# A seven-product block multiply on TensorE: two of the seven products in two matmuls per row block instead of three, and the sums of weights earlier

## Chip, cores, metric

The kernel runs on one core of a Trainium2 chip. The metric is the device time of one launch in microseconds, the median of several runs.

## What is computed

One decoder block in float32: a pre-norm, an input projection, latent attention and a gated spatial unit side by side, their gated sum, an output projection, and a SwiGLU feed-forward layer. Cut to the parts that the change touches, the products with the input projection's `u` and gate columns and with the two feed-forward weights:

```python
a = rms_norm(h, norm_mix_g[l])
z = a @ w_in[l]                 # 512 x 2048 times 2048 x 7232
...
f = rms_norm(h, norm_ffn_g[l])
h = h + (jax.nn.silu(f @ w_gate_ffn[l]) * (f @ w_up_ffn[l])) @ w_down_ffn[l]   # width 5632
```

## The kernel before

**Precision.** A float32 operand is split into a high part (rounded to the type `fp32r`, which TensorE multiplies in one pass) and a low part (the remainder). A product is then three matmuls: low weights by high data, high by high, high by low, summed in one PSUM bank.

**Units.** For `u`, the two gates, and the feed-forward gate and up weights, the work is cut into units of 256 output features by 512 tokens over 2048 inputs. A unit halves all three dimensions and does seven products of quarter size instead of eight (Strassen's scheme in Winograd's form). `Unit` (from line 400) holds a unit's weights `a11, a12, a21, a22`. For product `i`, `weights(i)` makes the sum or difference of quarters that it needs (`plus` and `minus`, lines 392 and 395, VectorE, 128x1024) and `form_w` splits it: ScalarE writes the high part (line 372), VectorE the low part (line 373). `multiply(i)` runs the product: `product` (lines 378 to 386) goes over 8 blocks of 128 rows, three matmuls of 256 columns each, 24 in a product. The data `x` of a block lies as 512 columns, high part first, low part behind it.

**Banks.** A unit has three PSUM banks of 512 columns, of which 256 are used. Products 0 to 6 add into banks 0, 1, 2, 1, 0, 1, 2. Between products, `read(i)` takes the sums so far:

- read 0: ScalarE copies bank 0 into `u` (line 398). Read 1: VectorE adds bank 1 and `u` into `u2` (line 392), before product 3 adds to bank 1 again.
- read 3: two VectorE adds, of bank 1 and of bank 2, into `c22`. Read 4: a ScalarE copy of bank 0. Read 5: an add of bank 1. Read 6: an add of bank 2, and then the unit is finished: SiLU for a gate unit of the feed-forward part (a multiply of two tiles on VectorE at line 908, the activation on ScalarE at line 909), a multiply with the gate for an up unit (line 916), an activation on ScalarE alone in the first run.

**Order.** `run` (from line 465) writes the order out by hand, and `pin` keeps it on each engine. Step `g` of the loop stands for product `g`: first `read` of product `g - 4`, then `weights` of product `g`, then `multiply` of product `g - 3`. So the weights are three products ahead of TensorE, and the reads one behind. Steps run on over the units: the reads of products 3 to 6 of a unit fall beside the weights of products 0 to 3 of the next. There are 20 units in the first run (4 of `u`, 8 pairs of the two gates) and 44 in the second (22 pairs of feed-forward gate and up).

**Buffers.** `Arena` (from line 46) hands out pieces of two large tiles, `af` (float32) and `ar` (the split parts), by rules of least recent use. The sum `s1` of a unit is a piece of `af` from product 1 to product 3.

Of the kernel before, what the change touches and what calls it, by code (L numbers as in the profile page):

```python
# [88 lines left out]
def tile_block(ctx: ExitStack, tc, a):  # L89
    nc = tc.nc  # L90
# [8 lines left out]
    def T():  # L99
        return af.get(2)  # L100

    def drop(*ts):

        for t in ts:
            if isinstance(t, (tuple, list)):
                drop(*t)
            elif id(t) in af.held:
                af.put(t)
            else:
                ar.put(t)  # L110

    def PS():
        return psp.tile([P, 512], F32, tag="b", name="b")
# [183 lines left out]
    kps = PS()  # L297
    for half in range(2):
# [5 lines left out]
        for k in range(8):  # L304
            w = wk[:, k].rearrange("p o m -> p (o m)")
# [61 lines left out]
    pin = tc.keep_in_program_order  # L367

    def form_w(src):
        hi, lo = ar.get(4), ar.get(4)  # L370
        hv, lv = (t.rearrange("p (k m) -> p k m", m=P) for t in (hi, lo))
        pin(nc.scalar.copy(hv, src))  # L372
        pin(nc.vector.tensor_tensor(out=lv, in0=src, in1=hv.bitcast(F32), op=ALU.subtract))  # L373
        return hi, lo

    FORM = (0, 5, 6, 4, 1, 2, 3)

    def product(ps, w, xs, kps, first):
        hi, lo = w
        for kp in kps:  # L380
            x = xs[kp]
            ks = slice(kp * P, (kp + 1) * P)
            xh, xl = x[:, :256], x[:, 256:]
            pin(nc.tensor.matmul(ps, lo[:, ks], xh, start=first and kp == 0, stop=False, skip_group_check=True))  # L384
            pin(nc.tensor.matmul(ps, hi[:, ks], xh, start=False, stop=False, skip_group_check=True))  # L385
            pin(nc.tensor.matmul(ps, hi[:, ks], xl, start=False, stop=kp == 7, skip_group_check=True))  # L386

    def bank():
        return PS()[:, :256]

    def plus(out, in0, in1):
        pin(nc.vector.tensor_tensor(out=out, in0=in0, in1=in1, op=ALU.add))  # L392

    def minus(out, in0, in1):
        pin(nc.vector.tensor_tensor(out=out, in0=in0, in1=in1, op=ALU.subtract))  # L395

    def copy(out, t):
        pin(nc.scalar.copy(out, t))  # L398

    class Unit:  # L400
# [8 lines left out]
            self.finish = finish  # L409

        def weights(self, i):
            if i == 0:
                return form_w(self.a11)
            if i == 1:
                self.st = af.get(4)
                self.s1 = self.st.rearrange("p (k m) -> p k m", m=P)
                plus(self.s1, self.a21, self.a22)
                minus(self.a21, self.a11, self.a21)
                minus(self.a11, self.s1, self.a11)
                return form_w(self.a11)  # L420
            if i == 2:
                return form_w(self.a21)
            if i == 3:
                w = form_w(self.s1)
                drop(self.st)
                return w
            if i == 4:
                return form_w(self.a12)
            if i == 5:
                minus(self.a12, self.a12, self.a11)  # L430
                return form_w(self.a12)
            w = form_w(self.a22)
            drop(self.raw)
            return w

        def multiply(self, i, w, fx, kps):
            if i == 0 and 0 in kps:
                self.banks = [bank() for _ in range(3)]
            n = FORM[i]
            xs = [f[n] if isinstance(f, list) else f[:, n * 512:(n + 1) * 512] for f in fx]  # L440
            product(self.banks[(0, 1, 2, 1, 0, 1, 2)[i]], w, xs, kps, i < 3)

        def read(self, i):
            ba, bb, bd = self.banks
            if i == 0:
                self.out = T(), T()
                self.u = T(), T()
                copy(self.u[0][:, :256], ba)
            u, u2 = self.u[0][:, :256], self.u[1][:, :256]
            (c11, c12), (c21, c22) = ((t[:, :256], t[:, 256:]) for t in self.out)  # L450
            if i == 1:
                plus(u2, bb, u)
            elif i == 3:
                plus(c22, bb, u)
                plus(c22, bd, c22)
            elif i == 4:
                copy(c11, ba)
            elif i == 5:
                plus(c12, bb, u)
            elif i == 6:  # L460
                plus(c21, bd, u2)
                drop(self.u)
                self.finish(self.out)

    def run(jobs, fx, rest, ends, lead=3):


        af.keep, af.pack = 32, True
        jobs = list(jobs)
        last = 7 * len(jobs) - 7  # L470
        units, ready = {}, {}

        def unit(n):
            if n < len(jobs):
                units[n] = Unit(*jobs[n])

        unit(0)
        for g in range(last + 7 + lead + 1):
            g1, g2 = g - lead, g - lead - 1
            if g2 >= 0:  # L480
                units[g2 // 7].read(g2 % 7)
            if g < last + 7:
                ready[g] = units[g // 7].weights(g % 7)
                if g % 7 == 6:
                    unit(g // 7 + 2)
            if g == lead - 1:
                rest = rest()
                next(rest)
                early = len(fx)
                for i in range(lead):  # L490
                    units[0].multiply(i, ready[i], fx, range(early))
                for _ in rest:
                    pass
                unit(1)
            if 0 <= g1 < last + 7:
                if g1 == last:
                    fx[:] = [ar.cut(f, 2) for f in fx]
                units[g1 // 7].multiply(g1 % 7, ready[g1], fx, range(early if g1 < lead else 0, len(fx)))
                drop(ready.pop(g1))
                if g1 >= last:  # L500
                    drop([f[FORM[g1 - last]] for f in fx])
                    if g1 - last in ends:
                        ends[g1 - last]()
        af.keep, af.pack, ar.keep = 0, False, 0
# [28 lines left out]
    def x_rest():  # L533
# [5 lines left out]

    latT, zs = [], []  # L540
    run(x_jobs(), fx, x_rest, {0: lambda: zs.append(lat_in(0)), 2: lambda: zs.append(lat_in(1)),
                               4: lambda: latT.append(latents(0, zs[0])), 5: lambda: latT.append(latents(1, zs[1]))})
    qnT, kvT = latT
# [119 lines left out]
    def k_proj(pr):  # L663
        ch = [chunk(a["w_ukv"][pr, c]) for c in range(2)]
        ks = []
        for m in range(2):
            ps = PS()
            for k in range(4):
                hi, lo = ch[k // 2]
                o = (k % 2) * 512 + m * P  # L670
                mm3(ps, hi[:, o:o + P], lo[:, o:o + P], *kvT[k], k == 0, k == 3)
            ks.append(split(ps))
        return ks, ch
# [63 lines left out]
    def values(e, pts, vs):  # L737
        ps = PS()
        for j, (ph, pl, q0) in enumerate(pts):
            vh, vl = vs[j // 2]  # L740
            o = (j % 2) * 256 + e * P
            mm3(ps[:, q0:], vh[:, o:o + P], vl[:, o:o + P], ph, pl, j == 0, j == NB - 1)
        return ps
# [15 lines left out]
    ks, ch = k_proj(0)  # L759
    vs = v_proj(ch)  # L760
    for pr in range(NP):
        prob, ptiles = scores(qs, qp, ks)
        if pr + 1 < NP:
            qs, qp = q_proj(pr + 1)
            ks, ch = k_proj(pr + 1)
# [12 lines left out]
        for e in range(2):  # L778
            ps = values(e, pts[e][1], vs)
            t = T()  # L780
# [60 lines left out]
    for c in range(4):  # L841
# [30 lines left out]
        if c == 0:  # L872
# [3 lines left out]
            for tb in range(NB):  # L876
                t = T()
# [56 lines left out]
    def split_hidden():  # L934
        hid[:4] = [move(t) for t in hid[:4]]

    run(ffn_jobs(), ff, f_rest, {1: lambda: hid.extend(hidden_in(0, 4)), 4: split_hidden,
                                 5: lambda: hid.extend(hidden(4, 4))})

# [32 lines left out]
    for c in range(4):  # L972
        t = T()
# [3 lines left out]
    for tb in range(NB):  # L977
        ts = slice(tb * P, (tb + 1) * P)
        for c in range(4):
            ps = PS()  # L980
            for k in range(4):
                xh, xl = hid[k]
# [6 lines left out]
        for c in range(4):  # L989
            t = h[tb][c]  # L990
# [87 lines left out]
```

## Time and profile before

| | |
|---|---|
| median of three runs | 2737.75 us (2736.56 to 2738.42) |
| the profiled execution | 2731.94 us |
| its span, first to last instruction | 2729.9 us |
| TensorE matmul busy | 2679.5 us, 98% of the span, 17320 matmuls |
| VectorE busy | 1731.3 us, 63% |
| ScalarE busy | 1093.6 us, 40% |
| mean granted TensorE clock | 0.993 |
| matmuls of lines 384, 385, 386 | 3584 each, mean 284 ns |
| other matmuls of the same kind, lines 169 to 171 | 2016 each, mean 379 to 380 ns |

The profile's times come from one profiled execution, so a sum made from them is set against 2731.94 us and then carried to the median. Busy time of an engine counts overlapping instructions once. A matmul's own duration holds its way through the array, and the next one starts before it ends: what a matmul costs in a stream is read from one start to the next. In a list of instructions the bracket at the end of a row is idle time of the engine just before it, and what ended it.

### The profile page before, as it was taken

To read this page: it belongs to the slowest core of one execution; us is meant where nothing else is said; L and a number is where in the kernel's file an instruction comes from. 1 tells how busy PE (TensorE), PEld (TensorE's weight loads), DVE (VectorE), ACT (ScalarE), POOL (GpSimd) and SP (SyncE) were. 2 spreads that over 40 slices of the span, in tenths; PEclk is the share of its full clock that TensorE was granted. 3 is DMA by queue.
4 is the path that set the end of the run, shared out by engine and by line. 5 is a ranking of instruction groups with operands and counts; after the bars stand their busy time and mean duration, and the time that the engine had idled before them with its cause. 6 is when DMAs were issued, how large, how long until landed. Compare 5 with 4: busy or idle time off the path is not lost.

```text
span 2729.9 us, 41675 instructions
## 1 busy us (share of the span) xinstructions
PE 2679.5 (98%) x17320; PEld 2458.8 (90%) x17320; DVE 1731.3 (63%) x2200; ACT 1093.6 (40%) x1534; POOL 201.4 (7%) x377
## 2 busy tenths in 40 slices
PE   8999999999899999999999999999999999999998
PEld 6879999998789878888799999999999998888887
DVE  5647777787677433333687887887888875344434
ACT  6334444457456422233544443444444343222212
POOL 1000000011101220001000000000000020000000
PEclk9999999999999999999999999999999999999999
DMA  7433343343423754334233232332322356334321
GB/s 300 150 125 114 119 146 125 130 144 129 139 86 124 250 188 147 120 112 139 101 123 118 110 131 109 131 111 107 140 109 109 132 170 224 123 123 132 112 89 62
DMA packets 104540, 365.22 MB, mean 134 GB/s; under 512 B 14304, under 2 KB 14304, under 8 KB 104352
## 3 DMA queue, kind: packets, MB, share of 16 engines
q1 hardware_dynamic: 72720, 260.60, 27.2%
q0 software_dynamic: 30192, 99.38, 10.6%
q8 instruction: 135, 2.21, 0.3%
q10 hardware_dynamic: 1440, 2.60, 0.3%
q14 instruction: 53, 0.43, 0.1%
HBM read 317.17 MB, written 45.35 MB: 133 GB/s over the span
## 4 chain that ended last, share of the span: by engine, by line
PE 82%; issue 9%; DMA 4%; DVE 3%; ACT 1%; POOL 1%; SPq 0%; POOLq 0%; ACTq 0%; DVEq 0%
PE b L384 15%; PE b L386 15%; PE b L385 15%; PE b L169 12%; PE b L171 12%; PE b L170 12%; DMA af<-in_xT 1%; DVE ar L373 1%; DMA af<-in_w_uq 1%; ACT ar L372 1%; DVE af L395 0%; PE b L732 0%; DVE af L392 0%; DMA sgd<-af 0%; DMA af<-in_w_lat 0%
## 5 line engine op out<-in xcount | busy, mean ns | idle before, releaser
L384 PE MATMUL b<-ar 128*128 128x256 f32 x3584 | 1017.6, 284 | 6.6 <-ACT ar L333 3.4
L386 PE MATMUL b<-ar 128*128 128x256 f32 x3584 | 1017.2, 284 | 5.4 <-DVE ar L119 5.4
L385 PE MATMUL b<-ar 128*128 128x256 f32 x3584 | 1016.5, 284 | 0.0
L169 PE MATMUL b<-ar 128*128 128x512 f32 (+1 forms) x2016 | 766.3, 380 | 25.3 <-ACT ar L154 11.6
L171 PE MATMUL b<-ar 128*128 128x512 f32 (+1 forms) x2016 | 763.8, 379 | 0.3 <-DVE ar L155 0.3
L170 PE MATMUL b<-ar 128*128 128x512 f32 (+1 forms) x2016 | 764.0, 379 | 0.0
L373 DVE TENSOR_TENSOR ar<-af,ar 128x1024 fp32r<-128x1024 f32 x448 | 543.2, 1223 | 267.9 <-ACT ar L372 266.9
L384 PEld LDWEIGHTS b<-ar 128*128 128x128 f32 x3584 | 690.5, 193 | 7.9 <-DVE af L392 4.0
L386 PEld LDWEIGHTS b<-ar 128*128 128x128 f32 x3584 | 690.5, 193 | 6.3 <-DVE ar L119 6.3
L385 PEld LDWEIGHTS b<-ar 128*128 128x128 f32 x3584 | 690.7, 193 | 0.1
L372 ACT CAST ar<-af 128x1024 fp32r<-128x1024 f32 x448 | 458.5, 1047 | 479.8 <-DVE af L395 367.9
L155 DVE TENSOR_TENSOR ar<-af,ar 128x1024 fp32r<-128x1024 f32 (+1 forms) x224 | 268.2, 1204 | 423.5 <-ACT ar L154 347.4
L169 PEld LDWEIGHTS b<-ar 128*128 128x128 f32 x2016 | 380.5, 189 | 97.6 <-ACT ar L154 11.9
L171 PEld LDWEIGHTS b<-ar 128*128 128x128 f32 x2016 | 380.2, 189 | 71.5 <-DVE ar L155 1.5
L170 PEld LDWEIGHTS b<-ar 128*128 128x128 f32 x2016 | 380.6, 189 | 69.6
L154 ACT CAST ar<-af 128x1024 fp32r<-128x1024 f32 (+1 forms) x224 | 230.0, 1036 | 503.0 <-PE b L170 241.6
L395 DVE TENSOR_TENSOR af<-af 128x1024 f32<-128x1024 f32 x192 | 234.6, 1222 | 4.3
L392 DVE TENSOR_TENSOR af<-b,af 128x256 f32<-128x256 f32 x320 | 134.3, 420 | 14.3 <-PE b L386 12.1
L137 ACT CAST ar<-af 128x512 fp32r<-128x512 f32 x100 | 59.6, 620 | 180.1 <-PE b L170 43.7
L398 ACT COPY af<-b 128x256 f32<-128x256 f32 x128 | 47.4, 370 | 178.8 <-PE b L386 132.5
L138 DVE TENSOR_TENSOR ar<-af,ar 128x512 fp32r<-128x512 f32 x100 | 67.2, 687 | 71.5 <-ACT ar L137 67.7
L942 DVE SCALAR_TENSOR_TENSOR af<-b,rest,af 128x512 f32<-128x512 f32 x96 | 71.3, 748 | 44.5 <-PE b L171 44.5
(223 smaller groups left out, 1193.5 us busy)
## 6 DMA issues: line engine op xcount, KB each, us to landing
af<-in_w_gate SPq DMA_DIRECT2D x88, 512.0 KB, 4.9
af<-in_w_up SPq DMA_DIRECT2D x88, 512.0 KB, 5.3
af<-in_w_down SPq DMA_DIRECT2D x88, 512.0 KB, 3.5
af<-in_w_g SPq DMA_DIRECT2D x64, 512.0 KB, 5.4
af<-in_w_oattn SPq DMA_DIRECT2D x32, 512.0 KB, 4.2
af<-in_w_out SPq DMA_DIRECT2D x32, 512.0 KB, 3.5
hidd<-af POOLq DMA_DIRECT2D x44, 256.0 KB, 2.6
af<-hidd POOLq DMA_DIRECT2D x44, 256.0 KB, 3.6
```

What stands on the lines that cost most here:

```text
L154: nc.scalar.copy(hi[:, :n], raw[:, :n])
L155: nc.vector.tensor_tensor(out=lo[:, :n], in0=raw[:, :n], in1=hi[:, :n].bitcast(F32), op=ALU.subtract)
L169: nc.tensor.matmul(ps, sl, mh, start=first, stop=False)
L170: nc.tensor.matmul(ps, sh, mh, start=False, stop=False)
L171: nc.tensor.matmul(ps, sh, ml, start=False, stop=last)
L372: pin(nc.scalar.copy(hv, src))
L373: pin(nc.vector.tensor_tensor(out=lv, in0=src, in1=hv.bitcast(F32), op=ALU.subtract))
L384: pin(nc.tensor.matmul(ps, lo[:, ks], xh, start=first and kp == 0, stop=False, skip_group_check=True))
L385: pin(nc.tensor.matmul(ps, hi[:, ks], xh, start=False, stop=False, skip_group_check=True))
L386: pin(nc.tensor.matmul(ps, hi[:, ks], xl, start=False, stop=kp == 7, skip_group_check=True))
L392: pin(nc.vector.tensor_tensor(out=out, in0=in0, in1=in1, op=ALU.add))
L395: pin(nc.vector.tensor_tensor(out=out, in0=in0, in1=in1, op=ALU.subtract))
```

## The change

For bank 2 (products 2 and 6) `product` takes the high weights once for both parts of the data, in one matmul of 512 columns, and then the low weights for the high part, 256 columns: two matmuls for a row block in place of three. The bank then holds two halves that have to be added, which `add`, new, does with one more VectorE add in read 3 and one in read 6. `u` and `u2` become the halves of one tile `us`. In `weights`, the three sums for products 1 to 3 are made in the step of product 0, and the difference for product 5 in the step of product 4, behind that step's split.

```diff
+    WIDE = (False, False, True)
+
+    def product(b, ps, w, xs, kps, first):
...
+            start, stop = first and kp == 0, kp == 7
+            if WIDE[b]:
+                pin(nc.tensor.matmul(ps, hi[:, ks], x, start=start, stop=False, skip_group_check=True))
+                pin(nc.tensor.matmul(ps[:, :256], lo[:, ks], xh, start=False, stop=stop, skip_group_check=True))
+            else:
+                ps = ps[:, :256]
...
         def weights(self, i):
...
             if i == 0:
-                return form_w(self.a11)
-            if i == 1:
+                w = form_w(self.a11)
                 self.st = af.get(4)
                 self.s1 = self.st.rearrange("p (k m) -> p k m", m=P)
                 plus(self.s1, self.a21, self.a22)
                 minus(self.a21, self.a11, self.a21)
                 minus(self.a11, self.s1, self.a11)
...
+            w = form_w((None, self.a11, self.a21, self.s1, self.a12, self.a12, self.a22)[i])
             if i == 3:
-                w = form_w(self.s1)
                 drop(self.st)
...
-            if i == 5:
+            elif i == 4:
                 minus(self.a12, self.a12, self.a11)
-                return form_w(self.a12)
...
+        def add(self, out, b, t=None):
+
+            ps = self.banks[b]
+            if t is not None:
+                plus(out, ps[:, :256], t)
+            if t is None and not WIDE[b]:
+                copy(out, ps[:, :256])
+            elif t is None:
+                copy(out, ps[:, 256:])
+                plus(out, ps[:, :256], out)
+            elif WIDE[b]:
+                plus(out, ps[:, 256:], out)
...
             if i == 0:
-                self.out = T(), T()
-                self.u = T(), T()
-                copy(self.u[0][:, :256], ba)
+                self.out, self.us = (T(), T()), T()
...
             elif i == 3:
-                plus(c22, bb, u)
-                plus(c22, bd, c22)
+                self.add(c22, 1, u)
+                self.add(c22, 2, c22)
...
             elif i == 6:
-                plus(c21, bd, u2)
-                drop(self.u)
+                self.add(c21, 2, u2)
+                drop(self.us)
```

In the changed file the wide matmul is line 389 and its narrow partner line 390, the other three are lines 393 to 395, `plus` is line 398, `minus` 401, `copy` 404.

TensorE, in a unit of the first run, from the end of product 1 to the start of product 2. `b_` with a number is a PSUM bank, `ar` holds the split parts. Before:

```order
L384 MATMUL b_2083<-ar_66 128x256
L385 MATMUL b_2083<-ar_66 128x256
L386 MATMUL b_2083<-ar_66 128x256
L384 MATMUL b_2084<-ar_66 128x256
L385 MATMUL b_2084<-ar_66 128x256
L386 MATMUL b_2084<-ar_66 128x256
```

and with the change:

```order
L393 MATMUL b_2027<-ar_66 128x256
L394 MATMUL b_2027<-ar_66 128x256
L395 MATMUL b_2027<-ar_66 128x256
L389 MATMUL b_2028<-ar_66 128x512
L390 MATMUL b_2028<-ar_66 128x256
```

Product 1 is as it was; a row block of product 2 is one matmul of 512 columns and one of 256.

VectorE, one turn of the loop in the first run, from the low forms of products 3 and 4 of a unit (`ar<-af,ar`) to read 6 of the same unit. Rows `af<-b,af` are adds out of PSUM, rows `af<-af` sums of weights. Before:

```order
L373 TENSOR_TENSOR ar<-af,ar 128x1024 x2
L392 TENSOR_TENSOR af<-b,af 128x256
L395 TENSOR_TENSOR af<-af 128x8x128
L373 TENSOR_TENSOR ar<-af,ar 128x1024 x2
L392 TENSOR_TENSOR af<-b,af 128x256 x2
L373 TENSOR_TENSOR ar<-af,ar 128x1024
L392 TENSOR_TENSOR af<-af 128x1024
L395 TENSOR_TENSOR af<-af 128x8x128 x2
L373 TENSOR_TENSOR ar<-af,ar 128x1024
L392 TENSOR_TENSOR af<-b,af 128x256
L373 TENSOR_TENSOR ar<-af,ar 128x1024
L392 TENSOR_TENSOR af<-b,af 128x256
```

and with the change:

```order
L373 TENSOR_TENSOR ar<-af,ar 128x1024 x2
L401 TENSOR_TENSOR af<-af 128x8x128
L398 TENSOR_TENSOR af<-b,af 128x256
L373 TENSOR_TENSOR ar<-af,ar 128x1024 x2
L398 TENSOR_TENSOR af<-b,af 128x256 x3
L373 TENSOR_TENSOR ar<-af,ar 128x1024
L398 TENSOR_TENSOR af<-af 128x1024
L401 TENSOR_TENSOR af<-af 128x8x128 x2
L373 TENSOR_TENSOR ar<-af,ar 128x1024
L398 TENSOR_TENSOR af<-b,af 128x256
L373 TENSOR_TENSOR ar<-af,ar 128x1024
L398 TENSOR_TENSOR af<-b,af 128x256 x2
```

The subtraction for product 5 and the add of read 1 have changed places; read 3 is three adds instead of two, read 6 two instead of one. The three sums of weights stand where they stood.

## Rows read from the trace of the kernel before

**Rows 1.** Busy time in 1400 to 2250 us: length, PE, PEld, DVE, ACT, POOL, clock, DMA.

```profile
1400.00:2250.00 850.00, 850.00 (x7053) 848.58 (x7053) 676.38 (x762) 354.57 (x431) 34.08 (x64) 1.00 0.34 123
```

**Rows 2.** Waits of the whole run: us in total, times, longest.

```profile
PE b L384 <- DVE af L392: 3.2, 3, 2.0
...
PE b L169 <- DVE nm L712: 9.5, 2, 7.7
...
ACT af L398 <- DVE ar L373: 43.3, 19, 3.6
```

**Rows 3.** TensorE in order of time, first run: start, duration; 49 matmuls left out.

```profile
599.78 0.28 PE L384 MATMUL b<-ar 128*128 128x256 f32 x1
...
605.78 0.28 PE L386 MATMUL b<-ar 128*128 128x256 f32 x1
```

**Rows 4.** The same in a stretch of 512 columns; 17 matmuls left out.

```profile
1099.74 0.39 PE L170 MATMUL b<-ar 128*128 128x512 f32 x1
...
1103.82 0.39 PE L170 MATMUL b<-ar 128*128 128x512 f32 x1
```

**Rows 5.** The same in attention, where the sizes change.

```profile
664.24 0.40 PE L169 MATMUL b<-ar 128*128 128x512 f32 x1
664.47 0.40 PE L170 MATMUL b<-ar 128*128 128x512 f32 x1
...
665.46 0.28 PE L169 MATMUL b<-ar 128*128 128x256 f32 x1
665.57 0.28 PE L170 MATMUL b<-ar 128*128 128x256 f32 x1
```

**Rows 6.** TensorE at an up unit: last matmul of one product 3, first of the next.

```profile
1970.89 0.28 PE L386 MATMUL b<-ar 128*128 128x256 f32 x1
...
1988.30 0.28 PE L384 MATMUL b<-ar 128*128 128x256 f32 x1
```

**Rows 7.** VectorE in the same stretch.

```profile
1971.21 0.88 DVE L392 TENSOR_TENSOR af<-b,af 128x256 f32<-128x256 f32 x2
1972.29 1.23 DVE L373 TENSOR_TENSOR ar<-af,ar 128x1024 fp32r<-128x1024 f32 x1 [0.20 <-ACT ar L372]
...
1980.95 0.41 DVE L392 TENSOR_TENSOR af<-b,af 128x256 f32<-128x256 f32 x1
...
1984.20 2.44 DVE L373 TENSOR_TENSOR ar<-af,ar 128x1024 fp32r<-128x1024 f32 x2 [1.64 <-ACT ar L372]
1986.56 0.42 DVE L392 TENSOR_TENSOR af<-b,af 128x256 f32<-128x256 f32 x1
1986.89 1.22 DVE L395 TENSOR_TENSOR af<-af 128x1024 f32<-128x1024 f32 x1
```

**Rows 8.** VectorE and TensorE in the first up unit, where product 3 waited.

```profile
1382.93 0.42 DVE L392 TENSOR_TENSOR af<-b,af 128x256 f32<-128x256 f32 x1
...
1382.43 0.28 PE L386 MATMUL b<-ar 128*128 128x256 f32 x1
1383.40 0.38 PE L384 MATMUL b<-ar 128*128 128x256 f32 x1 [0.69 <-DVE af L392]
1383.62 0.28 PE L385 MATMUL b<-ar 128*128 128x256 f32 x1
```

**Rows 9.** VectorE, ScalarE and TensorE (product 3) in the gate unit that follows.

```profile
2002.69 1.22 DVE L373 TENSOR_TENSOR ar<-af,ar 128x1024 fp32r<-128x1024 f32 x1
2004.25 1.22 DVE L373 TENSOR_TENSOR ar<-af,ar 128x1024 fp32r<-128x1024 f32 x1 [0.34 <-ACT ar L372]
...
2002.89 0.37 ACT L398 COPY af<-b 128x256 f32<-128x256 f32 x1 [1.77 <-PE b L386]
...
2008.45 0.28 PE L384 MATMUL b<-ar 128*128 128x256 f32 x1
```

**Rows 10.** VectorE (read 1) and TensorE (product 3) in a unit of the first run.

```profile
456.46 0.42 DVE L392 TENSOR_TENSOR af<-b,af 128x256 f32<-128x256 f32 x1
...
459.02 0.28 PE L384 MATMUL b<-ar 128*128 128x256 f32 x1
```

More of the change, by code (lines that the diff above doesn't have):

```diff
@@ L376, in tile_block @@
     FORM = (0, 5, 6, 4, 1, 2, 3)
-    def product(ps, w, xs, kps, first):
+    WIDE = (False, False, True)
+    def product(b, ps, w, xs, kps, first):
         hi, lo = w
@@ L383, in product @@
             xh, xl = x[:, :256], x[:, 256:]
[L384 to L389, printed above, removed]
+            start, stop = first and kp == 0, kp == 7
[4 more added lines that the diff above has]
+                ps = ps[:, :256]
+                pin(nc.tensor.matmul(ps, lo[:, ks], xh, start=start, stop=False, skip_group_check=True))
+                pin(nc.tensor.matmul(ps, hi[:, ks], xh, start=False, stop=False, skip_group_check=True))
+                pin(nc.tensor.matmul(ps, hi[:, ks], xl, start=False, stop=stop, skip_group_check=True))
     def plus(out, in0, in1):
@@ L419, in weights @@
                 minus(self.a11, self.s1, self.a11)
-                return form_w(self.a11)
-            if i == 2:
-                return form_w(self.a21)
+                return w
+            w = form_w((None, self.a11, self.a21, self.s1, self.a12, self.a12, self.a22)[i])
             if i == 3:
-                w = form_w(self.s1)
                 drop(self.st)
-                return w
-            if i == 4:
-                return form_w(self.a12)
-            if i == 5:
+            elif i == 4:
                 minus(self.a12, self.a12, self.a11)
-                return form_w(self.a12)
-            w = form_w(self.a22)
-            drop(self.raw)
+            elif i == 6:
+                drop(self.raw)
             return w
@@ L437, in multiply @@
             if i == 0 and 0 in kps:
-                self.banks = [bank() for _ in range(3)]
+                self.banks = [PS() for _ in range(3)]
             n = FORM[i]
             xs = [f[n] if isinstance(f, list) else f[:, n * 512:(n + 1) * 512] for f in fx]
-            product(self.banks[(0, 1, 2, 1, 0, 1, 2)[i]], w, xs, kps, i < 3)
+            b = (0, 1, 2, 1, 0, 1, 2)[i]
+            product(b, self.banks[b], w, xs, kps, i < 3)
+        def add(self, out, b, t=None):
[9 more added lines that the diff above has]
+                plus(out, ps[:, 256:], out)
         def read(self, i):
-            ba, bb, bd = self.banks
             if i == 0:
-                self.out = T(), T()
-                self.u = T(), T()
-                copy(self.u[0][:, :256], ba)
-            u, u2 = self.u[0][:, :256], self.u[1][:, :256]
+                self.out, self.us = (T(), T()), T()
+            u, u2 = self.us[:, :256], self.us[:, 256:]
             (c11, c12), (c21, c22) = ((t[:, :256], t[:, 256:]) for t in self.out)
-            if i == 1:
-                plus(u2, bb, u)
+            if i == 0:
+                self.add(u, 0)
+            elif i == 1:
+                self.add(u2, 1, u)
             elif i == 3:
-                plus(c22, bb, u)
-                plus(c22, bd, c22)
+                self.add(c22, 1, u)
+                self.add(c22, 2, c22)
             elif i == 4:
-                copy(c11, ba)
+                self.add(c11, 0)
             elif i == 5:
-                plus(c12, bb, u)
+                self.add(c12, 1, u)
             elif i == 6:
-                plus(c21, bd, u2)
-                drop(self.u)
+                self.add(c21, 2, u2)
+                drop(self.us)
                 self.finish(self.out)
```

## The prediction

> **What bounds the kernel now.** I read the busy time by stretch first. In the feed-forward half that runs as seven-product units, TensorE is busy 850.00 of 850 us at granted clock 1.00, and VectorE 676.38 us, 80% [rows 1]. So TensorE sets the end there, and VectorE has a fifth of the time in reserve, on the average only. The wait list agrees: in the whole run the first matmul of a product (line 384) waited on a PSUM read (line 392) three times, 3.2 us in all, and no PE wait is on the weight forms of lines 372 and 373 [rows 2]. There are 64 units, 20 in the first run and 44 in the feed-forward part (22 of gate, 22 of up, in turn).
>
> Two questions follow: what does TensorE gain, and does VectorE still deliver in time at each place where TensorE would wait for it?
>
> **The gain on TensorE.** A 256-column matmul is followed by the next after (605.78 - 599.78) / 50 = 0.120 us [rows 3], a 512-column one after (1103.82 - 1099.74) / 18 = 0.2267 us [rows 4]. Twice 0.120 is 0.240: doubling the columns costs 0.107, so 0.0133 us of each matmul is independent of its columns. Products 2 and 6 of a unit go from three matmuls per row block (0.360) to one of 512 and one of 256 (0.3467), 16 row blocks in a unit, 1024 in all: 1024 x 0.0133 = 13.7 us, 0.107 us per product and 0.213 us per unit of 20.16. No stretch alternates the two sizes. At the changes of size, a 512 after 256s took 0.23, and a 256 after longer ones 0.11 [rows 5]. A pair at 0.34 would save 20 ns, which is 20 us in all; nothing excludes 0.36, no saving. I take 13.7, from the long stretches; ends 0 and 20.
>
> The Trainium skill (TensorE: Matmul & The Clock Gate, section Back-to-back issue gap) gives N/2.4 + 2.5 ns for the spacing, so a matmul fewer would save 2.5 ns and the 1024 of them 2.6 us. The rows show 13.3 ns, five times as much; by that rule the sum below would end 11 us higher.
>
> **The reads cost VectorE more.** The wide bank holds two halves to be added, so read 3 and read 6 get one add each: 128 adds of 0.42 us, 54 us of VectorE. In total the reserve covers them. What matters is where they stand, and where the moved subtraction stands.
>
> Of the weight sums, the three of step 0 do not move on VectorE: they already stood directly behind the form of product 0. The subtraction for product 5 does move. Before, the order was low forms of products 3 and 4, the add of read 1, the subtraction. Now the subtraction is ahead of the add. That add reads bank 1, and product 3 of the same unit accumulates onto bank 1: it cannot start before the add has read. So 1.22 us of work is put ahead of something TensorE waits for.
>
> Up unit, in which the SiLU of the gate unit before it falls. The previous product 3 ends at 1970.89 + 0.28 = 1971.17, and this unit's product 3 starts at 1988.30 [rows 6]. VectorE does read 3 at 1971.21, the low form of product 0 at 1972.29 (after 0.20 of waiting for ScalarE), read 6 at 1980.95, low forms 3 and 4 from 1984.20, the add of read 1 at 1986.56 (ends 1986.98), the subtraction at 1986.89 [rows 7]. The margin now is 1988.30 - 1986.98 = 1.32 us. With the change:
> - read 3 has a third add. Two take 0.88, three some 1.32, so the form of product 0 starts at 1971.21 + 1.32 - 0.07 = 1972.46 (recorded spans overlap by about 0.07: 1986.98 against 1986.89), 0.17 later; the 0.20 of waiting takes the rest.
> - read 6 has a second add, 0.45 later; SiLU and the forms behind it follow, so all is 0.62 later.
> - the subtraction is at 1986.56 + 0.62 = 1987.18, the add 1.22 - 0.07 = 1.15 behind it at 1988.33, its end at 1988.75, and product 3 can start at 1988.80.
> - TensorE, with two narrower products in this stretch, would be ready at 1988.30 - 0.21 = 1988.09.
> So it waits 0.71 us. The trace holds one such wait: at 1382.93 to 1383.35 the add of read 1 ran late, and product 3 started at 1383.40, 0.05 after it; the matmul behind it came 0.22 later instead of 0.12 [rows 8]. With this 0.10 the wait costs 0.81 us. 22 up units: 17.8 us.
>
> Gate unit: no SiLU stands before its forms, so VectorE is earlier: low form 3 at 2002.69, the copy of bank 0 on ScalarE at 2002.89, low form 4 at 2004.25, product 3 at 2008.45 [rows 9]. But one thing is added. In the built program of the change, this copy writes where the sum s1 lay, in each of the 21 gate units from the second on, so it waits for low form 3 to have read s1. The trace knows this wait: line 398 waited on line 373 19 times, 43.3 us in all [rows 2]; before, it is every second unit of the first run and every second gate unit. With it: form 3 at 2002.69 + 0.6 = 2003.29, ends 2004.51; copy at 2004.55, 1.66 later than now; form 4 at 2004.25 + 1.66 = 2005.91; subtraction 2007.06, add 2008.21 to 2008.63, product 3 at 2008.68 instead of 2008.45 - 0.21 = 2008.24. With the 0.10: 0.54 us, times 21: 11.3 us.
>
> First run: there the finishing is on ScalarE alone. The add is at 456.46 and product 3 at 459.02 [rows 10]. Even 0.62 later, with 1.15 for the subtraction, the add ends at 458.65, before 459.02 - 0.21 = 458.81. I count no wait; the end for this is 0.2 us in each of 20 units, 4 us.
>
> A wait does not add up to a growing lag: product 3 then ends later too, and the forms of products 5 and 6, begun right after the subtraction, are done by about its end, so each unit starts its chain again from the end of product 3.
>
> **Sum.** 17.8 + 11.3 - 0.9 (the wait at 1383.40, 0.97 - 0.12, which is there already) = 28.2 us lost, 13.7 gained: 14.5 us slower. On the profiled execution's own 2731.94 us that is 2746.4; that execution stands 5.8 below the median of the runs, 2737.75, so for the median 2752.3; with 0.7, a small part of its end of 4, for the first run, **2753**. An error of 0.25 us in the place of the add moves 43 units by 11 us.
>
> **Rivals.**
> - Faster: VectorE keeps its margin, the subtraction runs while product 1 is still at work, and only the gain is left: 2737.75 - 13.7 = 2724. For it: three waits in 64 units today, a fifth of VectorE free. Against it: in the up unit the two forms end at 1984.20 + 2.44 = 1986.64 today, and product 1 ends at about 1988.30 - 24 x 0.12 + 0.16 = 1985.58, so there is no time left to hide the subtraction in. It decides if VectorE gets there 0.7 us earlier than I work out. Chance 0.13.
> - The copy in the gate units does not hold up form 4: only the up units wait, 2753 - 11.3 = 2742. Chance 0.09.
> - VectorE becomes the bound: the 0.84 us more per unit are carried from unit to unit and 0.3 us of lag is left in each of 43: 2753 + 13 = 2766. For it: forms 5 and 6 end just at the end of product 3. Chance 0.07.
> - The merge saves TensorE nothing: the pair costs 0.36, the upper end above. Then 2753 + 13.7 = 2767, and TensorE still waits. Chance 0.05. By the Trainium skill's rule above (same page and section) this case would end at 2764.
> The one long stall at the start of attention (7.7 us on line 712 [rows 2]) hangs on loads whose order changes slightly; I leave it as it is.
>
> **How the numbers follow.** The forecast has 0.66. Its own range is 2742 to 2764, from the 11 us; with the two cases on either side of it the range is 2741 to 2767, which leaves out the faster case. A measurement of this kernel can tell 0.2% (5.5 us) from no change: faster is below 2732.3, slower above 2743.2. Faster: the first rival, 0.13. Same: the second rival and a little of the forecast's lower end, 0.11. Slower: the rest, 0.76.
>
> **What would show it.** In the profile after: the 512-column line 389 followed after 0.227 and line 390 after 0.120; a wait of line 393 on the VectorE add of line 398, some 43 times, 0.4 to 0.8 us each and about 25 us in all, nearly all in the feed-forward part; up and gate units at some 20.7 and 20.5 us instead of 20.16; the copy of line 404 waiting on line 373 in gate units. If TensorE stays at 850 of 850 us there, the chain of VectorE was worked out wrong; if units are shorter than 19.95, the pitch was.

## The result, and the profile after

The changed kernel takes **2777.64 us** (median of 4, 2774.18 to 2781.42) against 2738.09 before: ratio 1.0149, 95% interval 1.0136 to 1.0161. It is slower, as forecast, but by 39.5 us instead of 15, and outside the range of 2741 to 2767. The profiled execution:

```profile
span 2778.9 us, 39875 instructions
...
PE 2693.3 (97%) x16296; PEld 2409.5 (87%) x16296; DVE 1787.5 (64%) x2328; ACT 1091.2 (39%) x1534; POOL 201.5 (7%) x377
```

Busy time by stretch (columns as in [rows 1]): most of the feed-forward units, then their start, then the start of the w_down stage.

```profile
1420.00:2220.00 800.00, 783.06 (x5862) 743.49 (x5861) 654.40 (x771) 318.31 (x385) 20.37 (x38) 1.00 0.32 116
...
1355.00:1420.00 65.00, 55.76 (x375) 52.36 (x374) 46.19 (x66) 28.91 (x39) 1.24 (x3) 0.87 0.31 117
...
2295.00:2325.00 30.00, 26.87 (x111) 21.42 (x110) 17.32 (x21) 11.54 (x15) 4.57 (x9) 0.94 0.83 292
```

The same two starts in the kernel before:

```profile
1345.00:1410.00 65.00, 59.60 (x472) 58.22 (x471) 49.88 (x69) 32.01 (x43) 1.09 (x3) 0.95 0.34 121
...
2250.00:2280.00 30.00, 30.00 (x134) 24.86 (x133) 19.46 (x23) 14.16 (x17) 7.09 (x14) 1.00 0.94 325
```

In the long stretch TensorE, which was busy 850 of 850 us [rows 1], now is 783 of 800, with VectorE at 82%. The two starts have longer pauses of TensorE, and the granted clock, a mean of the 2.4 GHz level and the 1.2 GHz one, is 0.87 instead of 0.95 and 0.94 instead of 1.00. Over the whole span it is 0.989 against 0.993.

Waits of the whole run, against [rows 2]:

```profile
PE b L393 <- DVE af L398: 29.4, 47, 3.5
...
ACT af L404 <- DVE ar L373: 76.4, 21, 3.9
```

TensorE around product 3 of a gate unit, and in the last two rows of the up unit that follows, against [rows 3 to 6]: start, duration, in brackets the wait.

```profile
1957.81 0.40 PE L389 MATMUL b<-ar 128*128 128x512 f32 x1
1958.04 0.28 PE L390 MATMUL b<-ar 128*128 128x256 f32 x1
1958.16 0.40 PE L389 MATMUL b<-ar 128*128 128x512 f32 x1
...
1960.28 0.40 PE L389 MATMUL b<-ar 128*128 128x512 f32 x1
1960.52 0.28 PE L390 MATMUL b<-ar 128*128 128x256 f32 x1
1961.09 0.39 PE L393 MATMUL b<-ar 128*128 128x256 f32 x1 [0.29 <-DVE af L398]
1961.32 0.28 PE L394 MATMUL b<-ar 128*128 128x256 f32 x1
...
1981.13 0.28 PE L390 MATMUL b<-ar 128*128 128x256 f32 x1
1981.98 0.38 PE L393 MATMUL b<-ar 128*128 128x256 f32 x1 [0.57 <-DVE af L398]
```

A row block of a wide product takes (1960.28 - 1957.81) / 7 = 0.353 us, not 0.3467. Product 3 of the gate unit starts 0.45 us later than the 0.12 after its forerunner (1961.09 - 1960.52 - 0.12), that of the up unit 0.73 (1981.98 - 1981.13 - 0.12). Those are the places and nearly the sizes forecast (0.44 and 0.71).

Stage by stage, from first matmul to first matmul in the two profiled executions: first run 420.1 to 423.8, attention 287.6 to 290.8, the 512-column products behind it 440.4 to 443.5, feed-forward units 898.5 to 931.9, w_down 478.5 to 483.8. Two thirds of the loss is in the feed-forward units: a **pair** of a gate and an up unit (start to start of its first SiLU, mean of 17 pairs) takes 41.51 us instead of 40.32, and 22 x 1.19 is 26.2 of the 39.5 us. Two SiLUs in a row, before:

```profile
1982.06 1.17 ACT L909 ACTIVATE af<-af 128x512 f32<-128x512 f32 x2 [2.80 <-DVE af L908]
...
2022.44 1.18 ACT L909 ACTIVATE af<-af 128x512 f32<-128x512 f32 x2 [2.81 <-DVE af L908]
```

and with the change:

```profile
1975.75 1.17 ACT L923 ACTIVATE af<-af 128x512 f32<-128x512 f32 x2 [3.26 <-DVE af L922]
...
2017.25 1.17 ACT L923 ACTIVATE af<-af 128x512 f32<-128x512 f32 x2 [3.26 <-DVE af L922]
```

### The profile page after: what moved, and what is told of

Same layout as the page of the kernel before. It is cut to its first block, busy times and chain, and to the rows that moved or that the text cites. A ratio compares the mean times of both kernels' runs of the same rounds, so it can differ in the third digit from the quotient of the medians.

```text
span 2778.9 us, 39875 instructions
## 1 busy us (share of the span) xinstructions
PE 2693.3 (97%) x16296; PEld 2409.5 (87%) x16296; DVE 1787.5 (64%) x2328; ACT 1091.2 (39%) x1534; POOL 201.5 (7%) x377
## 5 line engine op out<-in xcount | busy, mean ns | idle before, releaser
L393 PE MATMUL b<-ar 128*128 128x256 f32 x2560 | 733.9, 287 | 32.8 <-DVE af L398 29.4
L395 PE MATMUL b<-ar 128*128 128x256 f32 x2560 | 728.6, 285 | 5.4 <-DVE ar L119 5.4
L394 PE MATMUL b<-ar 128*128 128x256 f32 x2560 | 728.2, 284 | 0.0
L393 PEld LDWEIGHTS b<-ar 128*128 128x128 f32 x2560 | 494.5, 193 | 53.6 <-DVE af L398 45.5
L395 PEld LDWEIGHTS b<-ar 128*128 128x128 f32 x2560 | 495.1, 193 | 6.3 <-DVE ar L119 6.3
L394 PEld LDWEIGHTS b<-ar 128*128 128x128 f32 x2560 | 495.1, 193 | 0.1
L169 PEld LDWEIGHTS b<-ar 128*128 128x128 f32 x2016 | 381.1, 189 | 105.6 <-ACT ar L154 15.0
L171 PEld LDWEIGHTS b<-ar 128*128 128x128 f32 x2016 | 380.9, 189 | 72.6 <-DVE ar L155 2.4
L170 PEld LDWEIGHTS b<-ar 128*128 128x128 f32 x2016 | 381.3, 189 | 69.8
L389 PE MATMUL b<-ar 128*128 128x512 f32 x1024 | 368.8, 400 | 0.0
L390 PE MATMUL b<-ar 128*128 128x256 f32 x1024 | 288.3, 282 | 0.0
L389 PEld LDWEIGHTS b<-ar 128*128 128x128 f32 x1024 | 193.4, 189 | 41.3
L398 DVE TENSOR_TENSOR af<-b,af 128x256 f32<-128x256 f32 x448 | 188.6, 421 | 18.6 <-PE b L395 11.0
L390 PEld LDWEIGHTS b<-ar 128*128 128x128 f32 x1024 | 194.3, 190 | 0.0
```

The source lines that it names most:

```text
L169: nc.tensor.matmul(ps, sl, mh, start=first, stop=False)
L170: nc.tensor.matmul(ps, sh, mh, start=False, stop=False)
L171: nc.tensor.matmul(ps, sh, ml, start=False, stop=last)
L389: pin(nc.tensor.matmul(ps, hi[:, ks], x, start=start, stop=False, skip_group_check=True))
L390: pin(nc.tensor.matmul(ps[:, :256], lo[:, ks], xh, start=False, stop=stop, skip_group_check=True))
L393: pin(nc.tensor.matmul(ps, lo[:, ks], xh, start=start, stop=False, skip_group_check=True))
```

## The experiments

All were timed against the kernel before in the same session; its medians there were 2736.7 to 2737.8. In brackets behind a time stand its ratio to the kernel before and the 95% interval of that ratio. "Pair" is as above.

### Is it the subtraction ahead of the add?

**e1_sub_back**, from the changed kernel:

```diff
+            if i == 5:
+                minus(self.a12, self.a12, self.a11)
             w = form_w(...)
...
-            elif i == 4:
-                minus(self.a12, self.a12, self.a11)
```

> The changed kernel with one edit: the subtraction for product 5 goes back to where it stood before, behind the add of read 1. The order theory (that subtraction in front of the add is what product 3 waits for): the 0.73 and 0.45 us waits of product 3 go from nearly all FFN units, the unit period there falls from 20.75 to about 20.05, the FFN stage gives back 23 to 28 us, and its low-clock stretches at the entry go too; time 2738 less 7 (the pitch as the trace of after shows it) plus up to 8: 2731 to 2746. The rival, that the two extra adds a unit are what holds the banks: the waits stay at over half of their size, time above 2760.

Measured: 2778.71 us (1.0144, 1.0129 to 1.0160), no gain at all. Pair 41.70. The waits are there too:

```profile
PE b L393 <- DVE af L398: 27.2, 43, 3.1
```

They are longer than with the subtraction ahead, 0.57 and 0.81 us in gate and up units. The theory of the prediction falls.

**e2_order_only**, the other half, from the changed kernel:

```diff
-    WIDE = (False, False, True)
+    WIDE = (False, False, False)
```

> The changed kernel without the wide product (all seven products in the three-matmul form, one read of 256 columns for each bank), its early sums and the one tile for u kept. The order theory: product 3 waits as in after, 0.6 to 0.8 us in an up unit and 0.4 to 0.5 in a gate unit, period of a gate and up pair 41.4 to 41.8, time 2770 to 2790, so the wide bank is not what costs. The rival that the extra adds cost: under 0.2 us of wait a unit, time 2736 to 2748.

Measured: 2746.27 us (1.0033, 1.0022 to 1.0044). Pair 40.45, and four waits in place of 47:

```profile
PE b L393 <- DVE af L398: 7.8, 4, 3.1
```

With the subtraction ahead, but without the extra adds, product 3 hardly waits. What the order costs is below the list: once in a pair, in the up unit, product 3 starts just as the add of read 1 lets it, and the matmul behind it comes 0.22 us later instead of 0.12, as in [rows 8]:

```profile
1958.73 0.39 PE L393 MATMUL b<-ar 128*128 128x256 f32 x1
1958.95 0.28 PE L394 MATMUL b<-ar 128*128 128x256 f32 x1
```

That is the 0.1 us by which the pair is over 40.32, 2 to 3 us in 22 pairs. The whole kernel is 3.6 us above the kernel before with u in one tile (e10 below, 2742.71).

**e4_wide_only**, the changed kernel with all weight sums at their old places:

> The wide bank alone: all the sums of the weights (the three on product 1 too) stand where they stood before. The order theory with the one subtraction as its whole cost: same as the kernel with that subtraction put back, within 3 us (2731 to 2746). If the three early sums also cost, at the first run or at the FFN entry: faster than it by 3 to 10 us, down to 2728.

Measured: 2778.82 us, waits 27.2 us in 43, as e1. So with the wide product and its adds in place, none of the moved sums matters.

### Is it the length of VectorE's stream?

What the adds could do is seen in the changed kernel's VectorE from the add of read 1 in a gate unit to that of the up unit behind it; the last three rows are the pauses of the other half of the pair:

```profile
1960.63 0.41 DVE L398 TENSOR_TENSOR af<-b,af 128x256 f32<-128x256 f32 x1
1961.88 2.36 DVE L373 TENSOR_TENSOR ar<-af,ar 128x1024 fp32r<-128x1024 f32 x2 [0.83 <-ACT ar L372]
1964.28 1.34 DVE L398 TENSOR_TENSOR af<-b,af 128x256 f32<-128x256 f32 x3
...
1967.92 2.48 DVE L401 TENSOR_TENSOR af<-af 128x1024 f32<-128x1024 f32 x2
1971.57 1.23 DVE L373 TENSOR_TENSOR ar<-af,ar 128x1024 fp32r<-128x1024 f32 x1 [1.17 <-ACT ar L372]
...
1974.18 0.88 DVE L398 TENSOR_TENSOR af<-b,af 128x256 f32<-128x256 f32 x2
1974.97 1.28 DVE L922 TENSOR_TENSOR af<-af,rxb 128x512 f32<-128x512 f32 x2
1977.89 2.45 DVE L373 TENSOR_TENSOR ar<-af,ar 128x1024 fp32r<-128x1024 f32 x2 [1.63 <-ACT ar L372]
1980.37 1.23 DVE L401 TENSOR_TENSOR af<-af 128x1024 f32<-128x1024 f32 x1
1981.51 0.42 DVE L398 TENSOR_TENSOR af<-b,af 128x256 f32<-128x256 f32 x1
1982.79 2.36 DVE L373 TENSOR_TENSOR ar<-af,ar 128x1024 fp32r<-128x1024 f32 x2 [0.85 <-ACT ar L372]
...
1992.46 1.23 DVE L373 TENSOR_TENSOR ar<-af,ar 128x1024 fp32r<-128x1024 f32 x1 [1.17 <-ACT ar L372]
...
1999.72 1.23 DVE L373 TENSOR_TENSOR ar<-af,ar 128x1024 fp32r<-128x1024 f32 x1 [1.44 <-ACT ar L372]
```

and ScalarE beside it (the SiLU at 1975.75, shown above, stands between the first two rows):

```profile
1970.49 2.00 ACT L372 CAST ar<-af 128x1024 fp32r<-128x1024 f32 x2 [2.96 <-DVE af L401]
...
1976.83 1.03 ACT L372 CAST ar<-af 128x1024 fp32r<-128x1024 f32 x1
...
1998.37 0.37 ACT L404 COPY af<-b 128x256 f32<-128x256 f32 x1 [3.63 <-DVE ar L373]
1998.64 1.05 ACT L372 CAST ar<-af 128x1024 fp32r<-128x1024 f32 x1
```

VectorE never waits for TensorE here. Its only pauses are for high casts of ScalarE, 7.1 us in the pair, and the casts that it pauses for wait for VectorE: for a weight sum, or behind the SiLU, or behind the copy of u, which waits for a low form. (One of them, for product 5 of the gate unit, is released by TensorE, 0.09 us after its sum was ready.) That is, but for those 0.09 us, a closed loop of two engines. In e1, where the sum for product 5 stands behind the add, ScalarE's waits from 1420 to 2230 us show even this one gone:

```profile
ACT ar L372 <- DVE af L401: 277.8, 78, 4.3
...
ACT ar L372 <- PE b L395: 0.7, 1, 0.7
```

The loop's length, not a place in it, would then set the pair, and 2 adds a unit of 0.45 us lengthen it by 1.8. The runs below try this.

**e5_no_adds**, from e1:

```diff
-            elif WIDE[b]:
-                plus(out, ps[:, 256:], out)
```

> The kernel with the subtraction put back, less the two extra adds of a unit (the second column half of the wide bank is left out of c22 and c21, so this part of the computation is missing). The loop theory: a pair of a gate and an up unit takes 41.7 us in it because VectorE's stream in program order, with the ScalarE casts it waits for, is that long; without four adds of 0.45 us it is 39.9 and TensorE sets the pace again at 20.05 a unit: no steady waits of product 3, time 2738 less 7, 2728 to 2736. The rival, that the wide bank itself (its accumulation, or the ring of banks) brings the waits: a pair stays over 41 us, time over 2765.

Measured: 2735.28 us (0.9997, 0.9987 to 1.0006), pair 40.09. TensorE is busy throughout the stretch again:

```profile
1420.00:2220.00 800.00, 800.00 (x6065) 770.03 (x6064) 637.85 (x719) 330.83 (x400) 26.21 (x49) 1.00 0.33 120
```

128 adds out, 43.4 us off. Behind a first pair of 41.25 us three take 39.86, and only the later ones 40.09. I read the 39.86 as the loop's own pace, 1.84 below e1's pair, while VectorE catches up after the start.

**e7_before_adds**, from the kernel before:

```diff
                 plus(c22, bb, u)
+                plus(c22, bb, u)
...
                 plus(c21, bd, u2)
+                plus(c21, bd, u2)
```

> The kernel before, with one add of read 3 and the add of read 6 issued twice (the same values written again), and nothing else of the change: no wide product, old places of the sums. The loop theory: a pair goes from 40.32 to 41.3 to 41.7 us, product 3 waits in nearly every FFN unit, time 2738 plus 22 to 35: 2760 to 2773. The rival that the wide bank brings the waits: within 4 us of 2738.

Measured: 2765.19 us (1.0111, 1.0098 to 1.0125). No wide product, no moved sum, and product 3 waits 18.3 us in 34. So adds are enough to bring the waits. The pair is shorter than expected, 40.90, and alternates, 40.18 and 41.69. The copies of u on ScalarE show why; two in gate units, a pair apart:

```profile
1992.74 0.37 ACT L398 COPY af<-b 128x256 f32<-128x256 f32 x1 [4.04 <-PE b L386]
...
2031.37 0.38 ACT L398 COPY af<-b 128x256 f32<-128x256 f32 x1 [0.77 <-PE b L386]
```

One copy comes late and the next early. The late one starts 0.09 us after the end of low form 3 at 1992.65, as it does where the profile names that wait (e13 below), so I read the wait as one for the low form, although the row names TensorE. With u in two tiles, every second gate unit has it. That its place then goes round, and lies where s1 lay every second time, fits this and was not looked at in this kernel.

**e13_adds_one_tile**, from e7:

```diff
-                self.u = T(), T()
-                copy(self.u[0][:, :256], ba)
-            u, u2 = self.u[0][:, :256], self.u[1][:, :256]
+                self.u = T()
+                copy(self.u[:, :256], ba)
+            u, u2 = self.u[:, :256], self.u[:, 256:]
```

> The kernel before with the doubled adds and, besides, u in one tile. The doubled adds alone made a pair 40.90 us, the change 41.51. If the one tile makes up the rest (the copy of u then waits in every gate unit for a low form that reads where u is written, and the cast of the next step stands behind that copy): a pair of 41.4 to 41.8, time 2765 plus 14 to 20: 2776 to 2788. If the tile is harmless to the loop: a pair of 40.9, time 2765 to 2772.

Measured: 2773.67 us (1.0134, 1.0117 to 1.0150), pair 41.68, now every one alike, and each gate unit's copy waits for the low form:

```profile
1990.34 0.37 ACT L398 COPY af<-b 128x256 f32<-128x256 f32 x1 [4.04 <-DVE ar L373]
```

The pair is as expected, the total 2 us under its bounds. The kernel before, with two more adds and one tile, has the changed kernel's pair (e1's 41.70) without its wide product. The total hides a part of the tile's effect: from e7 to e13 the feed-forward units grow from 914.0 to 930.4 us, while the stages before them get shorter.

**e14_after_two_tiles**, the changed kernel with u in `(T(), T())` again:

> The changed kernel with u in two tiles as before, and nothing else. If the one tile is a part of the loop's length: a pair falls from 41.51 to 40.7 to 41.1, time 2777.6 less 9 to 20: 2757 to 2769. If it is harmless: a pair of 41.5, time 2774 to 2781.

Measured: 2772.59 us (1.0129, 1.0113 to 1.0145), pair 41.25, alternating 41.50 and 40.94. The direction is right and the alternation returns, but by the medians the tile is worth 5 us here, not 9 to 20, and the intervals overlap. In the profile the feed-forward units are 8.4 us shorter (923.5 for 931.9) and w_down 5.3, but the first run is 9.3 us longer (433.1 for 423.8). In this stretch the copy waits for a low form in 10 units only, and the pairs between them stay at 40.94, not at TensorE's 40.09.

**e8_cast_first** shortens the loop and keeps the adds. From the changed kernel: the high cast of a step is issued before the bank read of that step, so it no longer stands behind the SiLU and the copy (and the wide matmuls are grouped, as in e3 below).

```diff
+            low = units[g // 7].high(g % 7) if g < last + 7 else None
             if g2 >= 0:
                 units[g2 // 7].read(g2 % 7)
             if g < last + 7:
-                ready[g] = units[g // 7].weights(g % 7)
+                ready[g] = units[g // 7].weights(g % 7, low)
```

`high` issues the cast alone; `weights` begins with `w = low()`, the subtraction that makes the low part, and its sums follow as in the change.

> The changed kernel complete, with its extra adds and its early sums, grouped matmuls, and each high cast on ScalarE issued ahead of the bank read of its step (ahead of the SiLU and of the copies). The loop theory: the casts no longer stand behind the SiLU (1.6 us of VectorE idle in an up unit) and the u copy (1.4 us in a gate unit), so the stream of a pair is under 39 us and TensorE sets the pace at 19.94 a unit: 2738 less 13, 2720 to 2732, faster than before. If the length of the stream is only VectorE's own busy time, with the casts hidden: over 2760 still.

Measured: **2726.81 us** (0.9973, 0.9961 to 0.9985), pair 39.97, faster than both kernels. At the same places VectorE now pauses less, and once for TensorE:

```profile
1965.49 1.34 DVE L405 TENSOR_TENSOR af<-b,af 128x256 f32<-128x256 f32 x3 [0.92 <-PE b L402]
...
1979.42 1.23 DVE L375 TENSOR_TENSOR ar<-af,ar 128x1024 fp32r<-128x1024 f32 x1 [0.50 <-ACT ar L372]
```

The pause behind the SiLU is 0.50 instead of 1.63; the one behind the copy of u is gone. TensorE has no gap left, and VectorE is at 85% without being the bound:

```profile
1420.00:2220.00 800.00, 800.00 (x6085) 773.10 (x6084) 676.43 (x802) 327.72 (x402) 27.27 (x51) 1.00 0.33 120
```

**e12_cast_first_alternating**: the casts first and nothing else, 512 and 256 columns alternating as in the change.

> The changed kernel with one edit: each high cast on ScalarE is issued ahead of the bank read of its step; the wide product alternates 512 and 256 columns as in the change. The loop theory: no steady waits of product 3, a unit of 20.05 us in the FFN, and against the kernel that also groups the matmuls 64 units times 0.11, 7 us more: 2731 to 2737. If the order of the matmuls was what removed the waits: a pair over 41 us, over 2760.

Measured: 2734.16 us (0.9991, 0.9982 to 1.0000), pair 40.11. One move in the issue order takes 43.5 us off the changed kernel.

**e11_cast_first_no_wide**: e8 with `WIDE` all False.

> Casts first, early sums and one tile for u, with all seven products in the form of before (no wide bank, no extra adds). If the wide bank with grouped matmuls is what makes the cast-first kernel faster than before: a unit of 20.16, time 2736 to 2744, not faster than before. If the issue order of the casts is itself the gain: 2725 to 2733.

Measured: 2740.46 us (1.0013, 1.0002 to 1.0024), pair 40.32. Casts first bring nothing where the loop does not bind; e8's gain over before needs the wide product.

**e15_two_wide**: e8 with `WIDE = (True, False, True)`.

> The cast-first grouped kernel with bank 0 wide as well (products 0 and 4; two more adds a unit). TensorE's pace would be 39.5 a pair, a stream of that kernel plus four adds of 0.45 about 40. If the stream has the room: 2727 less 12, 2713 to 2720. If it becomes the bound: waits come back, a pair of 39.8 to 40.6, time 2722 to 2745. The loop theory says the second.

Measured: 2780.89 us (1.0157, 1.0141 to 1.0173), pair 41.55. The loop binds again, as its theory says, but by more than I gave. The waits show a reason: the new adds of bank 0 also wait for the ScalarE copy of its other half, which puts another step of ScalarE into the loop. No run takes this step out alone.

```profile
DVE af L405 <- ACT af L411: 134.0, 123, 2.3
...
PE b L400 <- DVE af L405: 36.7, 46, 3.1
```

### What the wide product gains

**e3_grouped**, from e1; in a wide product:

```diff
+            for kp in kps:
+                pin(nc.tensor.matmul(ps, hi..., xs[kp], ...))
+            for kp in kps:
+                pin(nc.tensor.matmul(ps[:, :256], lo..., xs[kp][:, :256], ...))
```

> As the kernel with the subtraction put back, and within the wide product all 512-column matmuls of a call stand first and its 256-column ones behind them. If what takes back half of the pitch gain is the change of size from each matmul to the next: 512 followed after 0.227, 256 after 0.120, pair 0.347 in place of 0.354, about 7 us less than the kernel with the subtraction put back. If it is the wide matmul itself, or the weight load of the next one: 512 then 256 stay at about 0.354 a pair on average and the time is the same within 2 us.

Measured: 2778.60 us, as e1: the loop set the pair, and no saving of TensorE could show. **e6_grouped_no_adds** repeats it without the adds.

> The same with the 512-column matmuls of a wide product ahead of its 256-column ones (and the same part of the computation missing). If alternating the sizes is what takes half of the pitch gain: a unit of 19.94 us, time 6 to 7 us below the kernel that alternates, 2721 to 2730. If not: as that kernel within 2 us. If the waits stay (the rival on the bank): over 2765.

Measured: 2731.46 us (0.9984, 0.9975 to 0.9993), 3.8 below e5, a little above the bounds; pair 39.97 against 40.09. With e8 against e12 (39.97 against 40.11) the order of the two sizes is worth 0.12 to 0.14 us a pair, about 4 us in 64 units. The medians of e8 and e12 differ by 7.4, the ratios by 0.0018 or 4.9 us. Grouping does not bring back the pace of the long stretches. In e6, a wide product's first eight matmuls, its other eight, and the next product:

```profile
1955.26 2.00 PE L385 MATMUL b<-ar 128*128 128x512 f32 x8
1957.10 1.12 PE L388 MATMUL b<-ar 128*128 128x256 f32 x8
1958.05 0.28 PE L397 MATMUL b<-ar 128*128 128x256 f32 x1
```

Eight of 512 columns take 1.84 us, 0.230 each where [rows 4] has 0.2267, and eight of 256 take 0.95, 0.119 each: 0.349 us a row block.

### The stage entries

**e10_before_one_tile**, the kernel before with u in one tile, as e13 without the adds:

> The kernel before with u in one tile of 512 columns in place of two half-used ones, and nothing else. If the one tile is what shifts the buffers at the stage entries: w_down 481 to 485 in place of 478.5, time 2740 to 2745. If it is harmless: within 2 us of before.

Measured: 2742.71 us (1.0020, 1.0010 to 1.0029), pair 40.32 as before. In its profile w_down takes 484.5 us instead of 478.5, with a pause of TensorE and a stretch at the lower clock near its start, as after:

```profile
2253.00:2283.00 30.00, 27.48 (x108) 21.71 (x107) 20.54 (x23) 14.13 (x17) 6.11 (x12) 0.89 0.92 325
```

**e9_two_tiles**, e8 with two tiles:

> The cast-first kernel with grouped matmuls, with u in two tiles as in the kernel before. If the stall of 2.8 us some 22 us into w_down and the half clock behind it, which after and all its variants with the wide product have and before has not, come from the buffers of the one tile: w_down 484.8 falls to 478.5 to 480, time 2720 to 2724. If not: w_down stays at 483 to 486, time 2725 to 2729.

Measured: 2729.88 us (0.9978, 0.9967 to 0.9988), not to be told from e8. w_down falls to 481.3, short of the expected 480, but the products behind attention grow from 318.6 to 323.5 us over the same 1392 matmuls. And e12, with one tile, has w_down at 479.2. So a change of buffers moves the pauses from stage to stage by some 5 us, and no rule for it was found.

## Why the prediction was wrong

**What bounds the kernel.** Right for before. The warning "on the average only" was right too, but I then looked for a place where VectorE is late, and the limit is a cycle.

**The gain of 13.7 us** was about twice too large. Without the loop in the way, a pair falls from 40.32 to 40.09 (e5), 0.115 us a unit, 7.4 us over 64 units; grouped it is 0.175 (e6), 11.2 us. The 0.3467 came from long stretches of one size; [rows 5] held a hint, the 0.23 of a 512 after 256s, that I did not take. The 32 row blocks of the wide products in a pair save 7 ns each alternating, 11 ns grouped. The Trainium skill (TensorE: Matmul & The Clock Gate, section Back-to-back issue gap) puts the gap of an isolated matmul at full clock at N/2.4 + 2.5 ns, from which I estimate a saving of 2.5 ns. The runs lie between it and the 13.3 ns of the long stretches.

**The subtraction ahead of the add** is the step that failed. "So 1.22 us of work is put ahead of something TensorE waits for" is true as an order and nearly free as a cost: order alone costs 0.1 us a pair (e2) where 0.81 and 0.54 us were priced, and putting it back gains nothing (e1, e4). What the runs show in its place is the loop of VectorE and ScalarE, lengthened by the extra adds and by the copy of u. The 0.71 and 0.44 us came out at 0.73 and 0.45 for this other reason, which is luck. A size that fits, at the place foreseen, did not show the cause.

**"A wait does not add up to a growing lag ... each unit starts its chain again from the end of product 3"** is the wrong sentence behind it. VectorE starts from its own last work and from casts that wait for it; in the rows above TensorE adds 0.09 us to that. The rival of VectorE as the bound, with 0.07 and 2766, was the mechanism. I priced it as a lag left over in each unit. Its price is the loop's length less TensorE's pace: 41.51 - 40.09 = 1.42 us a pair.

**The extra adds** were said to be covered by the reserve in total. They are the cost: taking them out of e1 saves 43.4 us (e5), 22 x (41.70 - 40.09) = 35.4 of it in the feed-forward units.

**The copy of u** waiting in each gate unit was foreseen, with its 21 times. Its share comes from the one tile: 8.5 us by medians on the kernel before with adds (e13 against e7), 5 us on the changed one (e14); in the feed-forward units alone 16.4 and 8.4 us.

**The stage entries** were not in the sum, which has only 0.7 us for the first run besides the pairs. By medians 39.5 - 26.2 = 13 us lie outside the steady pairs. One tile alone costs 5.7 us, outside the steady pairs too (e10). The clock's share was not in the sum either: the profiled execution of after has 60.9 us at the 1.2 GHz level, that of before 36.2, which is 12.4 us more of full-speed time, partly while TensorE paused anyway. How the 13 us divide over buffers and clock stays open.

**Where the number went wrong.** The waits, with the wrong cause, were nearly the right size: 28.2 us forecast, 22 x 1.42 = 31.2 measured. The other 21 us of the miss are 6.3 us of gain that did not come and some 15 us outside the pairs: 39.5 - 31.2 + 7.4 = 15.7, with 0.7 foreseen.

The steps add up by medians: before 2737.0, one tile 2742.7 (e10), wide product without adds, three sums early 2735.3 (e5), the adds 2778.7 (e1), the subtraction moved 2777.6 (after). The steps depend on their order: what the tile does to the loop shows only once the adds are there.

## What to carry to other kernels

An engine that is 80% busy can be the bound: where its pauses are for a second engine that waits for it in turn, add up the loop, pauses included, and compare that with the pace of the engine thought to be the bound; the difference to it, not the idle share, is the reserve. Three tests told the loop from a late instruction here: moving the suspected instruction back left the period as long (e1), moving it alone hardly lengthened it (e2), and adding work with no other change brought the waits (e7). The cheap remedy was order between the engines of the loop: issue what the other engine needs before what merely follows (here each cast ahead of the SiLU and the copy), and only then spend the reserve.

## What I had not expected of the hardware

Alternating matmuls of 512 and 256 columns cost more than either size in a row: 0.353 us for one of each, 0.349 in groups of eight (e6), where the long stretches give 0.3467 [rows 3, 4]. In the trace of after the 256 follows the 512 after 0.23 to 0.24 us, and the 512 follows the 256 after 0.12. Why was not tested.
